# Attention stage of a fused decoder step: low parts on VectorE, cache pages in pairs, prompt transposes one step later

## The chip, the cores and the metric

The kernel runs on one core of a Trainium2 chip. A core has TensorE (PE; its weight loads are listed as PEld), VectorE (DVE), ScalarE (ACT) and GpSimd (POOL), and the DMA queues that SyncE (SP), ScalarE and GpSimd issue to. The metric is the device time of one execution in microseconds.

## The reference, cut to what matters

One step of a two-layer decoder trunk, for a prompt of 512 tokens and for 8 sampled sequences of 8 tokens each, with the same weights. Layer 0 projects the normalised input into five parts; a gating MLP uses two of them, differential attention the other three:

```
p = h @ w_in                      # u, v (gating MLP), q, k, vb (4 heads x 128)
s1 = q[..., :64] @ k[..., :64].T  # two score maps per head
s2 = q[..., 64:] @ k[..., 64:].T
a  = softmax(s1) - lam * softmax(s2)
o  = rmsnorm(a @ vb, attn_subln) * (1 - lam_init)
```

The prompt attends causally to itself. Each sampled sequence attends to 1024 past tokens, whose keys and values lie in a paged cache (8 pages of 128 tokens for each of 8 sequences, found through a page table), and to its own new tokens. Then come an output projection, a SwiGLU, and layer 1 with a diagonal state space model, a GLU and another SwiGLU.

## The kernel before

All 576 tokens (512 prompt, 64 sample) lie along the free axis. A projection is a list of units; a unit is 128 output columns. Its fp32 weights are split into a high and a low part: ScalarE rounds the tile (`wh`, line 260), and VectorE or GpSimd subtracts that from the tile (`wl`, line 263). Each product is then three matmuls into `acc` (line 278): high by high, low by high, high by low. `Stream.splits` prepares two units ahead, and the set `GLO` names the units whose subtraction GpSimd does: unit 0 and units 6 to 27. Units 0 to 19 are the layer's input projection, 20 to 27 the half of the output projection that needs the MLP part, 28 to 35 the half that needs attention.

Attention is woven into this stream. Each unit's matmul loop yields some four times; at each yield the `Driver` ticks, and every side generator then advances by its pace: `sample_attn` by `SP0 = 1.9` steps a tick from unit 4 on, `prompt_attn` by one step from unit 10 on. What a generator emits in a step enters the program there; the framework then orders each engine's instructions by that program order and a plan of when their inputs are ready. Each engine works through its order in sequence.

`sample_attn` walks over `order`: key passes (`keys`) and value passes (`values`) for four pairs of sequences. GpSimd gathers pages (line 725), five ahead, into six buffers `pg`. A key page is transposed by TensorE into a bank `ktp` (line 780), copied to `kt` by ScalarE or VectorE in turn (lines 783, 785), and scored two pages later (`lag`, `LAG = 2`; line 761, `ssc`) in four 128x32 tiles of the array, one for each head. Each score takes eight matmul instructions, as fp32 matmuls are issued in two. A value page is multiplied in the same four tiles (line 847, `so`). `soft` makes the weights of a pair, `finish` the normed heads; `side_step` advances these every second page.

`prompt_attn` works on 16 blocks (4 heads, 4 row blocks): `probs` (scores `S`, masks, Exp), one step later `weights` (VectorE's `p`, lines 647 to 650, and then at once TensorE's transposes `AT`, line 653, and ScalarE's copy), one step later `values` (`O`), and after a head's last block `normed`, whose square is GpSimd's (line 667) and whose product with `sub_b` is VectorE's (line 672). `v_rows` applies Gelu to a part of `v` and transposes it into the banks `vtm` and `vts` (lines 908, 909).

All these small results share four PSUM banks; `acc` has four of its own.

Of the kernel before, what the change touches and what calls it, by code (L numbers as in the profile page):

```python
# [12 lines left out]
AF = mybir.ActivationFunctionType  # L13
ALU = mybir.AluOpType
AX = mybir.AxisListType

P = 128
# [12 lines left out]
LAG = 2  # L30
# [4 lines left out]
CUTS = ((0, 4), (4, 8))  # L35
KSPL = 3
NPIN = 4
GLO = frozenset((0, *range(6, 28)))
SP0, SP1, SP2, SP3 = 1.9, 1.0, 1.0, 1.0
FPARTS = ((0, 6), (6, 6), (12, 6), (18, 4))  # L40


# [35 lines left out]
def kernel(ctx, tc, I, O, stop=None, dbg=None):  # L78
    nc = tc.nc
    V, A, G, PE, SP = nc.vector, nc.scalar, nc.gpsimd, nc.tensor, nc.sync  # L80
# [30 lines left out]
    def bank(name, shape=(P, 512)):  # L111
        return ps.tile(list(shape), F32, tag="bank", name=nm(name))
# [20 lines left out]
    ident = const("ident", [P, P])  # L133
# [364 lines left out]
    sub_b = const("sub_b", [P, P])  # L498
# [126 lines left out]
    def prompt_attn(heads):  # L625
        def probs(h, i):
            n = P * (i + 1)
            es = []
            sums = small("sums", 2)
            for e in range(2):  # L630
                sp = bank("S")
                PE.matmul(sp[:, 0:n], lhsT=qT[h][64 * e:64 * e + 64, P * i:P * i + P],
                          rhs=kT[h][64 * e:64 * e + 64, 0:n], start=True, stop=True)
                V.tensor_tensor(sp[:, n - P:n], sp[:, n - P:n], cmask, op=ALU.add)
                m = small("m", 1)
                V.reduce_max(m, sp[:, 0:n], axis=AX.X)
                nmx = small("nmx", 1)
                V.tensor_scalar(nmx, m, -0.125, None, op0=ALU.mult)
                p = blk("p", (P, 512))
                A.activation(p[:, 0:n], sp[:, 0:n], AF.Exp, bias=nmx, scale=0.125, accum_out=sums[:, e:e + 1])  # L640
                es.append(p)
            return es, sums

        def weights(i, es, sums):
            n = P * (i + 1)
            rc = small("rc", 2)
            V.reciprocal(rc, sums)
            V.tensor_tensor(rc[:, 1:2], rc[:, 1:2], neglam, op=ALU.mult)
            V.tensor_scalar(es[1][:, 0:n], es[1][:, 0:n], rc[:, 1:2], None, op0=ALU.mult)
            V.scalar_tensor_tensor(es[0][:, 0:n], es[0][:, 0:n], rc[:, 0:1], es[1][:, 0:n], op0=ALU.mult, op1=ALU.add)  # L650
            tp = bank("AT")
            for j in range(i + 1):
                PE.transpose(tp[:, P * j:P * j + P], es[0][:, P * j:P * j + P], ident)
            at = blk("at", (P, 512))
            A.copy(at[:, 0:n], tp[:, 0:n])
            return at

        def values(h, i, at, o):
            op = bank("O")
            for j in range(i + 1):  # L660
                PE.matmul(op[:, 0:P], lhsT=at[:, P * j:P * j + P], rhs=Vh[h][:, j, :],
                          start=(j == 0), stop=(j == i))
            V.tensor_copy(o[:, P * i:P * i + P], op[:, 0:P])

        def normed(h, o):
            sq = blk("osq", (P, 512))
            G.tensor_tensor(sq, o, o, op=ALU.mult)
            ss = small("oss", 4)
            V.tensor_reduce(ss, sq.rearrange("p (i d) -> p i d", i=4), axis=AX.X, op=ALU.add)
            r = rstd_from(ss, 4, P)  # L670
            o4 = o.rearrange("p (i d) -> p i d", i=4)
            V.tensor_tensor(o4, o4, sub_b.unsqueeze(1).to_broadcast([P, 4, P]), op=ALU.mult)
            V.tensor_tensor(o4, o4, r.unsqueeze(2).to_broadcast([P, 4, P]), op=ALU.mult)

        def out(h, o):
            tp = bank("oTp")
            for i in range(4):
                PE.transpose(tp[:, P * i:P * i + P], o[:, P * i:P * i + P], ident)
            ao[4 + h] = split_to(h, slice(0, NP), tp)

        todo = [(h, i) for h in heads for i in range(4)]
        pr, at, o = {}, {}, {}
        for t in range(len(todo) + 6):
            if t < len(todo):
                pr[t] = probs(*todo[t])
                yield
            if 0 <= t - 1 < len(todo):
                at[t - 1] = weights(todo[t - 1][1], *pr.pop(t - 1))
                yield
            if 0 <= t - 2 < len(todo):  # L690
                h, i = todo[t - 2]
                if i == 0:
                    o[h] = blk("o", (P, 512))
                while Vh[h] is None:
                    yield
                values(h, i, at.pop(t - 2), o[h])
                if i == 3:
                    normed(h, o[h])
                yield
            if 0 <= t - 4 < len(todo) and todo[t - 4][1] == 3:  # L700
                h = todo[t - 4][0]
                out(h, o.pop(h))
                yield


    def sample_attn():
# [23 lines left out]
        todo = []  # L730
# [12 lines left out]
        sc, at, side_ = {}, {}, []  # L743
# [27 lines left out]
        def keys(bp):  # L771
            for c in range(2):
                for j in range(4):
                    for b2 in range(2):
                        if len(lag) == LAG:
                            score(*lag.pop(0))
                        pgt = page()
                        tp = bank("ktp")
                        for h in range(4):
                            PE.transpose(tp[:, P * h:P * h + P], pgt[:, P * h:P * h + P], ident)  # L780
                        kt = ablk("kt", (P, 512))
                        if b2 == 0:
                            A.copy(kt, tp)
                        else:
                            V.tensor_copy(kt, tp)
                        lag.append((bp, c, j, b2, kt))
                        yield
                    side_step()

        def soft(bp):  # L790
# [40 lines left out]

        def values(bp):
            while bp not in at:
                if lag:
                    score(*lag.pop(0))
                side_step()
                yield
            w = at.pop(bp)
            for b2 in range(2):
                b = 2 * bp + b2  # L840
                ob = bank("so")
                for j in range(8):
                    vp = page()
                    if lag:
                        score(*lag.pop(0))
                    for h in range(4):
                        PE.matmul(ob[32 * h:32 * h + 32, 0:P], lhsT=w[:, 64 * j + 16 * h:64 * j + 16 * h + 32],  # L847
                                  rhs=vp[:, P * h:P * h + P], start=(j == 0), stop=(j == 7), tile_position=(0, 32 * h))
                    if j % 2 == 1:
                        side_step()  # L850
                    yield
                A.copy(OS[b // 4][:, b % 4, :], ob[:, 0:P])
            if bp % 2 == 1:
                side_.append(finish(bp // 2))

        def finish(n):
            while "done" not in smp:
                yield
            o = OS[n]
            ob = bank("son")  # L860
            for j in range(4):
                b = 4 * n + j
                for h in range(4):
                    PE.matmul(ob[32 * h:32 * h + 32, P * j:P * j + P], lhsT=atn[:, b // 2, 16 * h:16 * h + 32],
                              rhs=smp["Vs"][:, h, :], start=True, stop=True, tile_position=(0, 32 * h))
                if j == 1:
                    yield
            V.tensor_tensor(o.rearrange("p a b -> p (a b)"), o.rearrange("p a b -> p (a b)"), ob, op=ALU.add)
            yield
            sq = ablk("osq", (P, 4, P))  # L870
            G.tensor_tensor(sq, o, o, op=ALU.mult)
            ss = small("oss", 4)
            V.tensor_reduce(ss, sq, axis=AX.X, op=ALU.add)
            G.tensor_tensor(o, o, sub_b.unsqueeze(1).to_broadcast([P, 4, P]), op=ALU.mult)
            r = rstd_from(ss, 4, P)
            V.tensor_tensor(o, o, r.unsqueeze(2).to_broadcast([P, 4, P]), op=ALU.mult)
            yield
            yield
            tp = bank("soT")
            for j in range(4):  # L880
                PE.transpose(tp[:, P * j:P * j + P], o[:, j, :], ident)
            for h in range(4):
                split_to(h, slice(NP + 32 * n, NP + 32 * n + 32), tp)
# [12 lines left out]
    def v_rows(f):  # L896
# [4 lines left out]
        yield  # L901
        gv = vT[f]
        A.activation(gv, gv, AF.Gelu_apprx_tanh)
        yield
        yield
        tp, tq = bank("vtm"), bank("vts")
# [1021 lines left out]
```

## Time and profile before

| | before |
|---|---|
| median of 3 runs | 1450.46 us (1450.17 to 1450.61) |
| the profiled execution | 1450.84 us, span 1449.1 us |
| busy over the span | PE 96%, PEld 91%, DVE 57%, ACT 33%, POOL 16% |
| mean granted clock of TensorE | 0.984 of full speed |

A span is what the trace covers; the profiled execution took 1.7 us more than its span. Busy shares are averages over stages with different limits. The end of a matmul is modelled and matmuls overlap, so the time that a group of them holds TensorE is read from one start to the next, not from their durations. A wait names the instruction that waited, and what ended its wait.

### The profile page before, as it was taken

To read this page: it belongs to the slowest core of one execution; us is meant where nothing else is said; L and a number is where in the kernel's file an instruction comes from. 1 tells how busy PE (TensorE), PEld (TensorE's weight loads), DVE (VectorE), ACT (ScalarE), POOL (GpSimd) and SP (SyncE) were. 2 spreads that over 40 slices of the span, in tenths; PEclk is the share of its full clock that TensorE was granted. 3 is DMA by queue.
4 is the path that set the end of the run, shared out by engine and by line. 5 is a ranking of instruction groups with operands and counts; after the bars stand their busy time and mean duration, and the time that the engine had idled before them with its cause. 6 is when DMAs were issued, how large, how long until landed. Compare 5 with 4: busy or idle time off the path is not lost. (4 is left out here: it accounts for less than half of the span.)

```text
span 1449.1 us, 27653 instructions
## 1 busy us (share of the span) xinstructions
PE 1392.5 (96%) x11382; PEld 1316.6 (91%) x11382; DVE 829.9 (57%) x1955; ACT 479.6 (33%) x860; POOL 232.8 (16%) x250
## 2 busy tenths in 40 slices
PE   7999999988999999999999979999999999999997
PEld 6878777868899999999998978999999999999997
DVE  6433456557689744987983478544444444444455
ACT  4233455442422123233322345433222222222234
POOL 2565656552200000000000110010000000000002
PEclk9999999999999999999999989999999999999999
DMA  7566544353332433454457485233223322322411
GB/s 240 168 196 193 172 146 134 110 183 106 96 85 66 146 88 79 138 164 123 143 144 218 128 259 183 67 88 85 62 74 98 92 66 81 88 81 70 114 59 66
DMA packets 223557, 177.37 MB, mean 122 GB/s; under 512 B 34060, under 2 KB 199752, under 8 KB 223432
## 3 DMA queue, kind: packets, MB, share of 16 engines
q1 hardware_dynamic: 206312, 136.01, 32.4%
q0 software_dynamic: 10880, 35.66, 8.2%
q10 hardware_dynamic: 6240, 3.93, 0.9%
q8 instruction: 90, 1.47, 0.4%
q14 instruction: 35, 0.29, 0.1%
HBM read 154.24 MB, written 25.53 MB: 124 GB/s over the span
## 5 line engine op out<-in xcount | busy, mean ns | idle before, releaser
L278 PE MATMUL acc<-hi,wh 128*128 128x288 f32 x2432 | 724.3, 298 | 9.3 <-ACT wh L260 3.1
L278 PE MATMUL acc<-hi,wl 128*128 128x288 f32 x2432 | 719.3, 296 | 1.5 <-DVE wl L263 1.4
L278 PE MATMUL acc<-lo,wh 128*128 128x288 f32 x2432 | 718.7, 296 | 0.5 <-DVE lo L228 0.5
L278 PEld LDWEIGHTS acc<-hi,wh 128*128 128x128 f32 x2432 | 458.2, 189 | 16.6 <-ACT hi L227 4.9
L278 PEld LDWEIGHTS acc<-hi,wl 128*128 128x128 f32 x2432 | 458.6, 189 | 3.1 <-DVE wl L263 2.4
L278 PEld LDWEIGHTS acc<-lo,wh 128*128 128x128 f32 x2432 | 458.8, 189 | 1.8 <-issue 1.0
L260 ACT CAST wh<-raw 128x1024 fp32r<-128x1024 f32 (+2 forms) x196 | 184.9, 945 | 594.8 <-PE acc L278 405.8
L263 DVE TENSOR_TENSOR wl<-raw,wh 128x1024 fp32r<-128x1024 f32 (+2 forms) x173 | 191.7, 1108 | 52.6 <-ACT wh L260 51.9
L1114 DVE TENSOR_TENSOR tu<-acc,rb 128x288 f32<-128x288 f32 x88 | 40.1, 456 | 124.7 <-PE acc L278 124.6
L278 PE MATMUL acc<-gxh,wh 128*128 128x288 f32 x320 | 102.3, 323 | 0.9 <-DVE proj L372 0.9
L991 POOL TENSOR_TENSOR acc<-acc,sq 128x576 f32<-128x576 f32 x18 | 26.8, 1489 | 460.8 <-ACT sq L983 460.8
L278 PE MATMUL acc<-gxl,wh 128*128 128x288 f32 x320 | 97.3, 305 | 0.0
L278 PE MATMUL acc<-gxh,wl 128*128 128x288 f32 x320 | 96.5, 304 | 0.6 <-DVE wl L263 0.6
L1104 DVE TENSOR_TENSOR tg<-acc,rb 128x288 f32<-128x288 f32 x88 | 40.0, 456 | 97.2 <-PE acc L278 96.2
L1124 DVE TENSOR_TENSOR x<-acc,x 128x288 f32<-128x288 f32 x96 | 43.8, 457 | 73.4 <-PE acc L278 73.0
L1834 POOL TENSOR_TENSOR sq<-sq,sq 128x288 f32<-128x288 f32 x12 | 9.6, 803 | 431.2 <-ACT sq L1830 431.2
L725 POOL DMA_INDIRECT pg<-in_cache_k_dram,pidx x64 | 61.9, 966 | 61.0 <-PE ktp L780 24.6
L725 POOL DMA_INDIRECT pg<-in_cache_v_dram,pidx x64 | 64.3, 1004 | 44.1 <-PE so L847 14.0
L278 PEld LDWEIGHTS acc<-gxh,wh 128*128 128x128 f32 x320 | 61.8, 194 | 8.8 <-issue 8.1
L278 PEld LDWEIGHTS acc<-gxl,wh 128*128 128x128 f32 x320 | 62.2, 195 | 1.9 <-issue 1.6
L278 PEld LDWEIGHTS acc<-gxh,wl 128*128 128x128 f32 x320 | 61.5, 193 | 1.9 <-DVE wl L263 0.8
L263 POOL TENSOR_TENSOR wl<-raw,wh 128x1024 fp32r<-128x1024 f32 (+1 forms) x23 | 46.8, 2035 | 39.0 <-ACT wh L260 38.7
(441 smaller groups left out, 1522.6 us busy)
## 6 DMA issues: line engine op xcount, KB each, us to landing
raw<-in_w_ffn_in_dram SPq DMA_DIRECT2D x88, 512.0 KB
raw<-in_w_ffn_out_dram SPq DMA_DIRECT2D x24, 768.0 KB
raw<-in_w_in_even_dram SPq DMA_DIRECT2D x10, 1024.0 KB
raw<-in_w_glu_dram SPq DMA_DIRECT2D x16, 512.0 KB
raw<-in_w_out_even_dram SPq DMA_DIRECT2D x8, 512.0 KB
dF<-Fn SPq DMA_DIRECT2D x16, 256.0 KB
dG<-gt SPq DMA_DIRECT2D x16, 256.0 KB
dL<-dZ SPq DMA_DIRECT2D x64, 64.0 KB
```

Of the source, the lines that this page charges most:

```text
L260: c = A.copy(hi[:, 0:nk], src)
L263: c = (lo_eng or V).tensor_tensor(lo[:, 0:nk], src, f32(hi[:, 0:nk]), op=ALU.subtract)
L278: PE.matmul(pts[hf], lhsT=w[:, k, :], rhs=x[:, c0:c1], start=(k == 0 and wi == 0), stop=(k == nk - 1 and wi == 2))
L725: G.indirect_dma_start(out=t, out_offset=None, in_=src, in_offset=bass.IndirectOffsetOnAxis(ap=pidx[:, 8 * b + j:8 * b + j + 1], axis=0))
L991: G.tensor_tensor(self.acc[:, 0:NT], self.acc[:, 0:NT], q, op=ALU.add)
L1104: V.tensor_tensor(half(t, hf), pt, half(stat.need(), hf), op=ALU.mult)
L1114: V.tensor_tensor(half(t, hf), pt, half(stat.need(), hf), op=ALU.mult)
L1124: V.tensor_tensor(half(nxt[m], hf), pt, half(cur[m], hf), op=ALU.add)
L1834: G.tensor_tensor(acc[h], acc[h], q, op=ALU.add)
```

## The change

`GLO` shrinks to unit 0, so VectorE makes the low parts of units 6 to 27. `SP0` becomes 0.95, and each step of `keys` and `values` handles two pages: `keys` first scores all that is in `lag`, then transposes two pages; `values` multiplies two pages before it yields. In `prompt_attn` the transposes leave `weights` for a function `turned` that runs one step later, and `values`, `normed` and `out` move one step back with it. The squares in `normed` and `finish` go from GpSimd to ScalarE, the product with `sub_b` in `finish` from GpSimd to VectorE. `v_rows` yields once more before its transposes.

```
-GLO = frozenset((0, *range(6, 28)))
-SP0, SP1, SP2, SP3 = 1.9, 1.0, 1.0, 1.0
+GLO = frozenset((0,))
+SP0, SP1, SP2, SP3 = 0.95, 1.0, 1.0, 1.0
...
             V.scalar_tensor_tensor(es[0][:, 0:n], es[0][:, 0:n], rc[:, 0:1], es[1][:, 0:n], op0=ALU.mult, op1=ALU.add)
+            return es[0]
+
+        def turned(i, e):
+            n = P * (i + 1)
             tp = bank("AT")
             for j in range(i + 1):
-                PE.transpose(tp[:, P * j:P * j + P], es[0][:, P * j:P * j + P], ident)
+                PE.transpose(tp[:, P * j:P * j + P], e[:, P * j:P * j + P], ident)
             at = blk("at", (P, 512))
             A.copy(at[:, 0:n], tp[:, 0:n])
             return at
...
         def normed(h, o):
             sq = blk("osq", (P, 512))
-            G.tensor_tensor(sq, o, o, op=ALU.mult)
+            A.activation(sq, o, AF.Square)
...
-        for t in range(len(todo) + 6):
+        for t in range(len(todo) + 7):
...
             if 0 <= t - 1 < len(todo):
-                at[t - 1] = weights(todo[t - 1][1], *pr.pop(t - 1))
+                we[t - 1] = weights(todo[t - 1][1], *pr.pop(t - 1))
+            if 0 <= t - 2 < len(todo):
+                at[t - 2] = turned(todo[t - 2][1], we.pop(t - 2))
                 yield
-            if 0 <= t - 2 < len(todo):
-                h, i = todo[t - 2]
+            if 0 <= t - 3 < len(todo):
+                h, i = todo[t - 3]
...
         def keys(bp):
             for c in range(2):
                 for j in range(4):
+                    while lag:
+                        score(*lag.pop(0))
                     for b2 in range(2):
-                        if len(lag) == LAG:
-                            score(*lag.pop(0))
                         pgt = page()
...
                         lag.append((bp, c, j, b2, kt))
-                        yield
+                    yield
                     side_step()
...
         def values(bp):
             while bp not in at:
-                if lag:
+                while lag:
                     score(*lag.pop(0))
...
                     vp = page()
-                    if lag:
+                    while lag:
                         score(*lag.pop(0))
...
                     if j % 2 == 1:
                         side_step()
-                    yield
+                        yield
...
             sq = ablk("osq", (P, 4, P))
-            G.tensor_tensor(sq, o, o, op=ALU.mult)
+            A.activation(sq, o, AF.Square)
...
-            G.tensor_tensor(o, o, sub_b.unsqueeze(1).to_broadcast([P, 4, P]), op=ALU.mult)
+            V.tensor_tensor(o, o, sub_b.unsqueeze(1).to_broadcast([P, 4, P]), op=ALU.mult)
...
         A.activation(gv, gv, AF.Gelu_apprx_tanh)
+        yield
         yield
         yield
```

## Rows read from the trace of the kernel before

**Rows 1.** The page, part 1: busy us, share of the span, instructions.
```profile
PE 1392.5 (96%) x11382; PEld 1316.6 (91%) x11382; DVE 829.9 (57%) x1955; ACT 479.6 (33%) x860; POOL 232.8 (16%) x250
```

**Rows 2.** Two stretches: length, busy us by engine, clock, DMA share, GB/s.
```profile
130.00:320.00 190.00, 177.84 (x1725) 141.43 (x1725) 100.06 (x334) 87.57 (x205) 115.83 (x105) 0.96 0.51 155
320.00:350.00 30.00, 25.27 (x205) 22.79 (x206) 26.28 (x85) 7.22 (x15) 10.08 (x9) 1.00 0.47 139
```

**Rows 3.** TensorE's waits from 70 to 400 us: total, times, longest.
```profile
PE so L847 <- DMA pg<-in_cache_v_dram,pidx: 4.0, 2, 3.5
PE vts L909 <- ACT p L640: 2.6, 1, 2.6
...
PE sh L944 <- issue: 2.0, 1, 2.0
...
PE AT L653 <- DVE p L650: 1.4, 1, 1.4
```

**Rows 4.** Timeline of TensorE, two stretches: start us, us, instructions merged.
```profile
166.07 0.29 PE L278 MATMUL acc<-gxl,wh 128*128 128x288 f32 x1
166.21 0.29 PE L278 MATMUL acc<-gxh,wl 128*128 128x288 f32 x1
166.43 0.43 PE L761 MATMUL ssc<-kt,Qz 128*32 128x128 f32 x8
166.79 0.66 PE L780 MATMUL ktp<-ident,pg 128*128 128x128 f32 x4
...
194.06 0.65 PE L847 MATMUL so<-pg,sat 128*32 128x128 f32 x16
194.63 0.40 PE L278 MATMUL acc<-gxh,wh 128*128 128x288 f32 x1
```

**Rows 5.** Timeline of TensorE: first and last of 63 score runs, 44 value runs.
```profile
55.67 0.43 PE L761 MATMUL ssc<-kt,Qz 128*32 128x128 f32 x8
...
122.06 0.43 PE L847 MATMUL so<-pg,sat 128*32 128x128 f32 x8
...
258.21 0.40 PE L761 MATMUL ssc<-kt,Qz 128*32 128x128 f32 x8
...
319.31 0.43 PE L847 MATMUL so<-pg,sat 128*32 128x128 f32 x8
```

**Rows 6.** Three stretches with a lower granted clock (third figure from the right).
```profile
200.00:208.00 8.00, 8.00 (x49) 7.07 (x51) 1.73 (x5) 2.10 (x11) 1.93 (x2) 0.57 0.30 83
272.00:280.00 8.00, 8.00 (x41) 7.81 (x39) 0.70 (x1) 2.09 (x5) 1.29 (x1) 0.57 0.24 70
306.00:310.00 4.00, 3.04 (x18) 2.67 (x19) 0.00 (x0) 0.00 (x0) 3.08 (x4) 0.57 1.01 378
```

**Rows 7.** Timeline from 192 us, VectorE and GpSimd.
```profile
192.27 3.32 DVE L672 TENSOR_TENSOR o<-o,sub_b 128x512 f32<-128x512 f32 x1
192.64 2.40 POOL L263 TENSOR_TENSOR wl<-raw,wh 128x1024 fp32r<-128x1024 f32 x1
```

**Rows 8.** Groups by shape, 60 to 420 us: busy us, mean ns, idle before.
```profile
L263 POOL TENSOR_TENSOR wl<-raw,wh 128x1024 fp32r<-128x1024 f32 x14 | 33.5, 2390 | 7.3 <-ACT wh L260 7.1
L263 POOL TENSOR_TENSOR wl<-raw,wh 128x512 fp32r<-128x512 f32 x8 | 11.0, 1374 | 19.8 <-ACT wh L260 19.8
...
L263 DVE TENSOR_TENSOR wl<-raw,wh 128x1024 fp32r<-128x1024 f32 x6 | 7.3, 1222 | 2.4 <-ACT wh L260 2.4
L263 DVE TENSOR_TENSOR wl<-raw,wh 128x512 fp32r<-128x512 f32 x8 | 5.5, 694 | 0.1
L672 DVE TENSOR_TENSOR o<-o,sub_b 128x512 f32<-128x512 f32 x4 | 5.4, 1342 | 0.0
```

**Rows 9.** Timeline of GpSimd from 299 us.
```profile
300.09 1.30 POOL L263 TENSOR_TENSOR wl<-raw,wh 128x512 fp32r<-128x512 f32 x1
```

**Rows 10.** Groups by shape, 0 to 60 us: ScalarE's square over 128x512.
```profile
L404 ACT ACTIVATE junk<-xt 128x512 f32<-128x512 f32 x6 | 3.9, 643 | 0.0
```

**Rows 11.** Timeline of ScalarE's queue from 316 us.
```profile
335.26 5.36 ACTq L1263 DMA_DIRECT2D dZ<-zz x7
```

More of the change, by code (lines that the diff above doesn't have):

```diff
@@ L37 @@
 NPIN = 4
-GLO = frozenset((0, *range(6, 28)))
-SP0, SP1, SP2, SP3 = 1.9, 1.0, 1.0, 1.0
+GLO = frozenset((0,))
+SP0, SP1, SP2, SP3 = 0.95, 1.0, 1.0, 1.0
 FPARTS = ((0, 6), (6, 6), (12, 6), (18, 4))
@@ L650, in weights, with turned @@
             V.scalar_tensor_tensor(es[0][:, 0:n], es[0][:, 0:n], rc[:, 0:1], es[1][:, 0:n], op0=ALU.mult, op1=ALU.add)
+            return es[0]
+        def turned(i, e):
+            n = P * (i + 1)
             tp = bank("AT")
             for j in range(i + 1):
-                PE.transpose(tp[:, P * j:P * j + P], es[0][:, P * j:P * j + P], ident)
+                PE.transpose(tp[:, P * j:P * j + P], e[:, P * j:P * j + P], ident)
             at = blk("at", (P, 512))
@@ L666, in normed @@
             sq = blk("osq", (P, 512))
-            G.tensor_tensor(sq, o, o, op=ALU.mult)
+            A.activation(sq, o, AF.Square)
             ss = small("oss", 4)
@@ L681, in prompt_attn @@
         todo = [(h, i) for h in heads for i in range(4)]
-        pr, at, o = {}, {}, {}
-        for t in range(len(todo) + 6):
+        pr, we, at, o = {}, {}, {}, {}
+        for t in range(len(todo) + 7):
             if t < len(todo):
@@ L687, in prompt_attn @@
             if 0 <= t - 1 < len(todo):
-                at[t - 1] = weights(todo[t - 1][1], *pr.pop(t - 1))
+                we[t - 1] = weights(todo[t - 1][1], *pr.pop(t - 1))
+            if 0 <= t - 2 < len(todo):
+                at[t - 2] = turned(todo[t - 2][1], we.pop(t - 2))
                 yield
-            if 0 <= t - 2 < len(todo):
-                h, i = todo[t - 2]
+            if 0 <= t - 3 < len(todo):
+                h, i = todo[t - 3]
                 if i == 0:
@@ L695, in prompt_attn @@
                     yield
-                values(h, i, at.pop(t - 2), o[h])
+                values(h, i, at.pop(t - 3), o[h])
                 if i == 3:
@@ L699, in prompt_attn @@
                 yield
-            if 0 <= t - 4 < len(todo) and todo[t - 4][1] == 3:
-                h = todo[t - 4][0]
+            if 0 <= t - 5 < len(todo) and todo[t - 5][1] == 3:
+                h = todo[t - 5][0]
                 out(h, o.pop(h))
@@ L773, in keys @@
                 for j in range(4):
+                    while lag:
+                        score(*lag.pop(0))
                     for b2 in range(2):
-                        if len(lag) == LAG:
-                            score(*lag.pop(0))
                         pgt = page()
@@ L786, in keys @@
                         lag.append((bp, c, j, b2, kt))
-                        yield
+                    yield
                     side_step()
@@ L833, in values @@
             while bp not in at:
-                if lag:
+                while lag:
                     score(*lag.pop(0))
@@ L843, in values @@
                     vp = page()
-                    if lag:
+                    while lag:
                         score(*lag.pop(0))
@@ L850, in values @@
                         side_step()
-                    yield
+                        yield
                 A.copy(OS[b // 4][:, b % 4, :], ob[:, 0:P])
@@ L870, in finish @@
             sq = ablk("osq", (P, 4, P))
-            G.tensor_tensor(sq, o, o, op=ALU.mult)
+            A.activation(sq, o, AF.Square)
             ss = small("oss", 4)
             V.tensor_reduce(ss, sq, axis=AX.X, op=ALU.add)
-            G.tensor_tensor(o, o, sub_b.unsqueeze(1).to_broadcast([P, 4, P]), op=ALU.mult)
+            V.tensor_tensor(o, o, sub_b.unsqueeze(1).to_broadcast([P, 4, P]), op=ALU.mult)
             r = rstd_from(ss, 4, P)
@@ L903, in v_rows @@
         A.activation(gv, gv, AF.Gelu_apprx_tanh)
+        yield
         yield
```

## Prediction

> **What bounds the kernel.** I read the page first. TensorE is busy 96% of the span [rows 1], so only work that leaves its queue, or time in which it stands still, can pay. What the change touches runs from about 60 to 350 us; what comes later is the same code. The table of stretches [rows 2] shows three kinds of loss there. From 130 to 350 us TensorE stands idle for 190.00 - 177.84 + 30.00 - 25.27 = 16.9 us. Its clock is 0.96 in the first of the two. And GpSimd is busy 115.83 of 190 us, while VectorE has 100 of 190 and then 26.28 of 30: the only place where an engine beside TensorE is nearly full.
>
> The list of waits [rows 3] says what the larger stops wait for. `so` waits 4.0 us for a value page, `vts` 2.6 us for an Exp, `sh` 2.0 us for nothing that the list can name, `AT` (the prompt transposes) 1.4 us for the weights `p`. That is 10 us of the 16.9; the rest are stops under a microsecond.
>
> The timeline [rows 4] shows a loss that no wait shows, because TensorE counts as busy in it. Full-array matmuls start 0.14 us apart, but a group of scores (128x32 tiles) after one starts 0.22 us behind it: 0.08 to enter. A group of eight (one page) holds the queue 166.79 - 166.43 = 0.36 us, a group of sixteen (two pages) 194.63 - 194.06 = 0.57. Eight more cost 0.21, so 0.15 of the 0.36 is leaving. One trip into the small tiles and back is 0.08 + 0.15 = 0.23 us.
>
> **Pages in pairs.** How many trips? In the timeline of the whole stage the 64 pages' scores stand in 63 runs and the 64 value pages in 44; [rows 5] shows the first and the last run of each. A few touch one another, which leaves 102 trips with the few other small-tile runs. After the change a step scores two pages and then transposes two, and a value step takes two. Halving the pace to 0.95 keeps pages per tick. That makes 32 + 32 trips, and I add 4 for the small runs of `soft` and `finish`: 68, 34 fewer, 34 x 0.23 = 7.8 us off. Bounds: if only the key pages pair up (63 to 35), 28 x 0.23 = 6.4; if neighbours also merge (102 to 58), 10.1. I take 7.8, as value pages already ran in sixteens at times.
>
> [...]
>
> **Low parts off GpSimd.** 22 of the 23 subtractions on GpSimd go to VectorE: 14 of 2.390 us and 8 of 1.374 [rows 8], 44.5 us. On VectorE the same shapes take 1.222 and 0.694 [rows 8]: 17.1 + 5.6 = 22.7 us added. What this removes beyond GpSimd's time stands in [rows 7]: VectorE's product with `sub_b` took 3.32 us while GpSimd worked from 192.64 to 195.04. The four of that group average 1.342 [rows 8], so the other three took (4 x 1.342 - 3.32) / 3 = 0.68. The 2.6 us lost held up the next masks and Exp, which held the bank that `vts` needed: this is the 2.6 us wait of [rows 3]. Behind it the granted clock falls to half; the 8 us stretch at 200 us has a mean of 0.57 [rows 6], so 8 x 0.43 = 3.4 us are lost. Together 6.0 us hang on it. VectorE's and ScalarE's order around it will also change, and a bank must still be waited for; bounds 0 and 6.0, I take 4.
>
> [...]
>
> The value page: at 300.09 a subtraction of 1.30 us [rows 9] stands in GpSimd's queue ahead of the gathers that follow, and a page that TensorE then lacks makes the longest stop of [rows 3], 3.5 of the 4.0 us, with a half clock behind it (4 x 0.43 = 1.7 us, [rows 6]). Without the subtraction those gathers go 1.3 us earlier; bounds 0 and 4.0 + 1.7 = 5.7, I take 1.3. I leave the `sh` stop and its clock (2.0 + 3.4, [rows 3, 6]) as it is: nothing in the change speaks to its cause. Bounds 0 and 5.4.
>
> **What VectorE pays.** It is covered by TensorE's matmuls up to 320 us, where VectorE has 90 of 190 us free. Two things can uncover it. A subtraction must wait for ScalarE's cast, and in VectorE's queue the page copies `kt`, the score masks and the evacuations of `acc` stand behind it, and TensorE behind those. The six in [rows 8] waited 2.4 us in all, 0.4 each; 22 would wait 8.8 us of VectorE. And from 320 to 350 us VectorE is 88% busy; if all eight half-size subtractions fall there they add 8 x 0.69 = 5.6 us, and one `sub_b` product 0.7. Bounds 0 and 6.3 + 8.8 = 15; I take 2, since the same GpSimd instructions also stretched VectorE there.
>
> **Squares on ScalarE.** Six squares of 0.64 us [rows 10], 3.9 us, where ScalarE has more than half of 190 us free [rows 2]. Late in the stage there is one trap: ScalarE's queue issues transfers for 5.36 us from 335.26 [rows 11], and a square queued behind them would hold the last head's norm, its transposes and the projection units that need them. Bounds 0 and 5.4; I take 0.5, as TensorE still has other projection units there.
>
> **Transposes a step behind.** The instructions are the same 40 transposes and 16 copies; the wait on `p`, 1.4 us [rows 3], goes. The weights now live one step longer, in a ring of 44 buffers; heads finish one step later, but the number of steps with a yield stays 52. Bounds: 1.4 off, and one step put on at the end, 190 / 52 = 3.7 us if the 52 steps fill the long stretch of [rows 2]. I take 1 off. The extra yield in `v_rows` gives Gelu one step more and moves nothing else; 0, bounds as for the wait on `vts` above.
>
> **Banks.** A key step now wants two banks at once for its transposes, out of four. Lower bound 0; upper, every one of 32 pairs waits for a copy of 0.69 us (the VectorE pass above), 22 us. At a pace of 1.9 a tick already sends two pages through these banks, so I take 1.
>
> **Sum.** -7.8 - 4 - 1.3 - 1 + 2 + 0.5 + 1 = -10.6 us. The profiled execution took 1450.84 us, 1449.1 of it span and 1.7 around it; the median is 1450.46, 0.4 less. 1450.46 - 10.6 = 1439.9; I say **1440**.
>
> **Rivals.**
> 1. The forecast: 1430 to 1447 us, chance 0.55. The trips go and some stops with them.
> 2. The trips go but are given back, in VectorE's last 30 us, behind casts or in a new stop with its half clock: 15 us at most against 14.1 off, so about 1448 to 1452; or the pairs are pulled apart in the instruction order, which leaves the trips and, -10.6 + 7.8 = -2.8, gives 1447.7. For it: VectorE at 88% [rows 2]; against it: 90 us free before. Chance 0.22, three quarters of it above 1447.6.
> 3. Slower: the pair's two banks. With the prompt's scores holding others, the second set of transposes waits for a copy, and TensorE, which works in order, with it. The pairs win 10.6 us in all, so from 10.6 / 32 = 0.33 us a pair on this turns the sign; at 0.69 us a pair it is 1450.5 - 11.6 + 22 = 1461. For it: four banks for all; against it: in [rows 4] the transposes start directly behind the scores. Chance 0.13.
> 4. All the stops named above go as well, with their half clocks: 7.8 + 6.0 + 5.7 + 5.4 + 1.4 = 26 us, 1424. Chance 0.10, mostly between 1424 and 1432.
>
> Faster by over 0.2% (2.9 us, about what a measurement of this kernel can tell from none) means under 1447.6: 0.55 + 0.10 and a quarter of rival 2, 0.70. Within it 0.15, slower 0.15. The range from 1428 to 1452 leaves out most of rival 3 and the end of rival 4; the likeliest case alone has 1430 to 1447.
>
> **What would show it.** Right: scores and values in groups of sixteen, key transposes in eights, near 68 trips; the four `sub_b` products of the prompt all near 0.69 us; one subtraction left on GpSimd; no wait of `AT` on `p`; the projection units that end at 350 us ending near 340. Wrong: as many trips as before, transposes that wait for a `kt` copy, TensorE's idle time from 320 us on growing, or new half-clock stretches. The prediction is most open to the last: a stop of 2 us costs 3.4 more in clock, and where stops fall I can't derive.

## The result and the profile after

The changed kernel takes 1436.82 us (median of 4 runs, 1430.29 to 1438.41) beside 1450.53 for the kernel before (4 runs, 1450.17 to 1451.69): a ratio of 0.9894, 95% interval 0.988 to 0.9909, 13.7 us. A second set of runs (e12 below, on chip 11; the chip of the first set is not on record) gave 1428.39 beside 1445.25, ratio 0.989 [0.9868, 0.9912], 16.9 us. The forecast was 1440 with a range from 1428 to 1452; the rest of this text is about whether its terms were the right ones. The kernel before took 1449.82 us on chip 2 and 1444.64 and 1445.25 on chip 11, so a time is always set against the kernel before of its own set.

The page of the changed kernel, part 1 [against rows 1]:

```profile
PE 1384.8 (97%) x11382; PEld 1317.7 (92%) x11382; DVE 840.3 (59%) x1979; ACT 482.8 (34%) x866; POOL 182.3 (13%) x220
```

GpSimd has 50 us less to do and VectorE only 10 us more, though it took over 44.5 us of GpSimd's subtractions. The stretches of rows 2 in the changed kernel, and before them the one that holds the half clock that is left, 0.50 from 298 to 300 us (length, busy us by engine, clock, DMA share, GB/s):

```profile
296.00:304.00 8.00, 8.00 (x55) 5.40 (x58) 4.22 (x11) 2.27 (x7) 3.15 (x4) 0.79 0.55 168
130.00:320.00 190.00, 181.63 (x1827) 146.91 (x1824) 117.48 (x379) 94.73 (x220) 87.23 (x90) 0.99 0.54 165
320.00:350.00 30.00, 29.67 (x225) 29.30 (x224) 24.53 (x75) 10.26 (x17) 2.86 (x2) 1.00 0.37 115
```

TensorE's idle time from 130 to 350 us is 8.37 + 0.33 = 8.7 us; it was 16.9 [rows 2]. From 130 to 320 us its clock is 0.99 instead of 0.96. The low stretches at 200 and 272 us [rows 6] are gone, and the one at 306 has become 8 us at 0.79. Behind 350 us the clock is no better: its mean from 350 to 420 us is 0.95, and was 0.98. The last transposes `rbp` ahead of the SwiGLU, which both programs have, start at 378.19 us instead of 394.74; the spans of the two profiled executions differ by 14.2 us, so 2.4 of these 16.6 us are lost again later.

TensorE's waits from 70 to 400 us [against rows 3]:

```profile
PE so L853 <- issue: 3.0, 3, 2.3
PE so L853 <- DMA pg<-in_cache_v_dram,pidx: 2.7, 3, 1.0
...
PE AT L657 <- ACT p L640: 1.8, 1, 1.8
PE rowt L464 <- ACT S L772: 1.4, 2, 0.7
```

The waits of `vts` on an Exp, of `sh`, and of `AT` on VectorE's `p` are gone; no wait for a page is longer than 1.0 us. Not all is better: `so` now stands 3.0 us for nothing that the list can name, and `AT` waits 1.8 us for an Exp. New is `rowt`, which waits until ScalarE has copied the score bank `S` out. Timeline of TensorE [against rows 4 and 5]:

```profile
162.27 0.64 PE L767 MATMUL ssc<-kt,Qz 128*32 128x128 f32 x16
162.85 1.09 PE L786 MATMUL ktp<-ident,pg 128*128 128x128 f32 x8
...
184.38 0.65 PE L767 MATMUL ssc<-kt,Qz 128*32 128x128 f32 x16
184.84 0.62 PE L853 MATMUL so<-pg,sat 128*32 128x128 f32 x16
```

Scores come in sixteens and transposes in eights, directly behind them. Counted over the stage there are 73 trips into the small tiles, 29 fewer than the 102 before. Groups by shape from 60 to 420 us [against rows 8 and 10]:

```profile
L263 DVE TENSOR_TENSOR wl<-raw,wh 128x1024 fp32r<-128x1024 f32 x23 | 28.1, 1223 | 5.1 <-ACT wh L260 4.2 <-issue 0.5
...
L263 DVE TENSOR_TENSOR wl<-raw,wh 128x512 fp32r<-128x512 f32 x16 | 11.0, 688 | 1.2 <-ACT wh L260 1.2
...
L676 DVE TENSOR_TENSOR o<-o,sub_b 128x512 f32<-128x512 f32 x4 | 2.7, 682 | 0.0
...
L671 ACT ACTIVATE osq<-o 128x512 f32<-128x512 f32 x4 | 2.5, 628 | 0.6 <-DVE rsy L180 0.6
```

All four products with `sub_b` take 0.68 us; the one of 3.32 [rows 7] is gone. VectorE's idle time before all 39 subtractions is 6.3 us; the prediction's upper bound was 8.8 us for 22 of them.

### The profile page after: what moved, and what is told of

Read it like the earlier page. It is cut to its first block, busy times and chain, and to the rows that moved or that the text cites. A ratio compares the mean times of both kernels' runs of the same rounds, so it can differ in the third digit from the quotient of the medians.

```text
span 1434.9 us, 27625 instructions
## 1 busy us (share of the span) xinstructions
PE 1384.8 (97%) x11382; PEld 1317.7 (92%) x11382; DVE 840.3 (59%) x1979; ACT 482.8 (34%) x866; POOL 182.3 (13%) x220
## 5 line engine op out<-in xcount | busy, mean ns | idle before, releaser
L263 DVE TENSOR_TENSOR wl<-raw,wh 128x1024 fp32r<-128x1024 f32 (+2 forms) x195 | 214.1, 1099 | 56.1 <-ACT wh L260 54.4
L227 ACT CAST hi<-tu 128x576 fp32r<-128x576 f32 x44 | 29.8, 677 | 41.9 <-DVE tu L1123 41.9
```

The source lines that it names most:

```text
L227: A.copy(hi, src)
L263: c = (lo_eng or V).tensor_tensor(lo[:, 0:nk], src, f32(hi[:, 0:nk]), op=ALU.subtract)
```

## The experiments

In the first four, theory A is the prediction's (the saved trips bring most of the gain), theory B that the work taken off GpSimd does. e1 to e4 ran on chip 2, all later ones on chip 11.

**e1, pairs alone.** The kernel before with the new `keys` and `values` and `SP0 = 0.95`.

```
-SP0, SP1, SP2, SP3 = 1.9, 1.0, 1.0, 1.0
+SP0, SP1, SP2, SP3 = 0.95, 1.0, 1.0, 1.0
...
+                    while lag:
+                        score(*lag.pop(0))
                     for b2 in range(2):
-                        if len(lag) == LAG:
-                            score(*lag.pop(0))
```

> The kernel before with the pairs and the pace of 0.95 alone. In its instruction order the small-tile trips fall from 102 to 71. Theory A (a trip costs TensorE 0.23 us whatever else happens): 31 x 0.23 = 7.1 us off, about 1443.4 us, with the stop of vts and its half clock perhaps still there. Theory B (the trips lie in time that TensorE would have waited anyway, and the gain came from GpSimd's work leaving): within 2 us of 1450.5.

1463.4 us beside 1449.82, ratio 1.0087 [1.0067, 1.0107]: 13.6 us slower, which neither theory said. It makes 71 trips, 31 fewer than before, and gives back more than they save. Where? The stretches of the kernel before (first fence) and of e1:

```profile
60.00:130.00 70.00, 69.16 (x724) 56.78 (x724) 22.12 (x56) 23.63 (x42) 44.39 (x42) 1.00 0.59 176
```

```profile
60.00:130.00 70.00, 63.31 (x686) 56.49 (x684) 20.82 (x47) 21.33 (x36) 39.68 (x37) 0.98 0.53 165
130.00:320.00 190.00, 168.14 (x1633) 136.74 (x1634) 101.53 (x333) 87.40 (x205) 109.28 (x100) 0.94 0.47 146
320.00:350.00 30.00, 26.13 (x259) 20.68 (x259) 18.01 (x56) 7.37 (x18) 17.02 (x17) 0.96 0.54 168
```

TensorE idles 6.7 us from 60 to 130 (0.8 before) and 21.9 + 3.9 = 25.7 from there to 350 (16.9 before), and its clock is lower in all three. There are two kinds of stop. The first, in e1's timeline of several engines from 82 us, happens three times:

```profile
82.21 0.66 PE L761 MATMUL ssc<-kt,Qz 128*32 128x128 f32 x16
...
82.80 1.09 PE L780 MATMUL ktp<-ident,pg 128*128 128x128 f32 x8
...
83.73 0.60 PE L462 MATMUL rows<-ident,proj 128*128 128x128 f32 x4
...
84.08 0.38 PE L278 MATMUL acc<-gxh,wh 128*128 128x288 f32 x1
85.31 0.69 DVE L764 TENSOR_REDUCE mx<-ssc 128x1 f32<-128x512 f32 x1 [2.92 <-PE acc L278]
...
86.04 0.59 ACT L766 COPY S<-ssc 128x512 f32<-128x512 f32 x1 [4.54 <-issue]
...
86.68 0.42 PE L464 MATMUL rowt<-ident,proj 128*64 128x128 f32 x1 [2.21 <-ACT S L766]
```

`ssc`, two `ktp` and `rows` hold the four banks, so `rowt` waits for the score bank: reduced by VectorE, then copied by ScalarE. The reduction starts 2.4 us after the scores' end. VectorE was idle for 2.92 us up to it, and by its line a signal of TensorE ended this wait (`PE acc`). Five groups of TensorE, the scores first and one `acc` last, end between 82.87 and 84.46 us by the modelled ends, and neither VectorE nor ScalarE starts anything until 85.31. So the reduction was late with TensorE's signal; why that came so long after the modelled ends is not shown. The second kind, in e1's timeline around 250 us, VectorE, GpSimd and TensorE in this order:

```profile
249.50 0.69 DVE L873 TENSOR_REDUCE oss<-osq 128x4 f32<-128x512 f32 x1 [1.16 <-POOL osq L871]
...
250.47 3.78 DVE L186 TENSOR_SCALAR var<-oss 128x4 f32<-128x4 f32 x1
...
256.35 0.28 DVE L663 COPY o<-O 128x128 f32<-128x128 f32 x1
```

```profile
250.63 1.29 POOL L874 TENSOR_TENSOR OS<-OS,sub_b 128x512 f32<-128x512 f32 x1
251.87 2.34 POOL L263 TENSOR_TENSOR wl<-raw,wh 128x1024 fp32r<-128x1024 f32 x1
```

```profile
251.65 0.29 PE L278 MATMUL acc<-gxh,wh 128*128 128x288 f32 x1
256.69 0.72 PE L908 MATMUL vtm<-ident,proj 128*128 128x128 f32 x4 [4.75 <-DVE o L663]
```

A VectorE instruction over four columns, 0.16 us in the changed kernel, takes 3.78 us and ends 0.04 us after the two GpSimd instructions that run beside it. The copy of `O` stands behind it and eleven short instructions, and `vtm` waits for that copy's bank: TensorE stands for 4.75 us.

**e2, the GpSimd work moved and nothing else.** Low parts, squares and products, in the kernel before.

```
-GLO = frozenset((0, *range(6, 28)))
+GLO = frozenset((0,))
...
-            G.tensor_tensor(sq, o, o, op=ALU.mult)
+            A.activation(sq, o, AF.Square)
...
-            G.tensor_tensor(o, o, sub_b.unsqueeze(1).to_broadcast([P, 4, P]), op=ALU.mult)
+            V.tensor_tensor(o, o, sub_b.unsqueeze(1).to_broadcast([P, 4, P]), op=ALU.mult)
```

> The kernel before with the low parts, squares and the sub_b product off GpSimd alone; trips 105. Theory A: +0.7 for three trips, -5.3 for the stops of vts and of the value page, +2.5 for VectorE and ScalarE: about 1448 us. Theory B: most of the 13.7 us, 1440 us or less.

1434.45 us beside 1449.82, ratio 0.9891 [0.9871, 0.9911]: 15.4 us, as much as the whole change, with as many trips as before (105). B. Its stretches:

```profile
130.00:320.00 190.00, 183.00 (x1823) 145.66 (x1823) 119.88 (x389) 94.75 (x220) 89.32 (x88) 0.99 0.52 161
320.00:350.00 30.00, 29.73 (x220) 29.41 (x219) 21.49 (x64) 10.03 (x16) 2.60 (x2) 0.96 0.43 133
```

Idle time 7.00 + 0.27 = 7.3 us, 9.6 less than before [rows 2]; the clock of the first goes from 0.96 to 0.99, 5.7 us, and that of the second to 0.96, 1.2 us the other way. 9.6 + 5.7 - 1.2 = 14.1 of the 15.4, an estimate from these rows. VectorE is busy 119.88 us in the long stretch instead of 100.06, and the wait of `vts` on an Exp is gone from e2's list.

**e3, the later transposes alone.** `turned` and the extra yield of `v_rows` in the kernel before.

```
-                at[t - 1] = weights(todo[t - 1][1], *pr.pop(t - 1))
+                we[t - 1] = weights(todo[t - 1][1], *pr.pop(t - 1))
+            if 0 <= t - 2 < len(todo):
+                at[t - 2] = turned(todo[t - 2][1], we.pop(t - 2))
```

> The kernel before with the prompt's transposes one step later and the extra yield alone; trips 100. Theory A: the 1.4 us wait of AT goes and two trips with it, about 1449 us. Theory B: the same; a gain of over 4 us would speak for neither, but for the step as the cause.

1445.87 us beside 1449.82, ratio 0.9969 [0.9957, 0.9981]: 4.0 us faster, where both theories said about 1449. The waits of `AT` on VectorE are gone from its list of waits, and so is that of `vts`: though GpSimd still makes the low parts, none of the four products with `sub_b` is stretched here (0.68 us on average). So the 4.0 us are not those of the wait on `p` alone.

**e4, pairs pulled apart again.** The changed kernel, but a key step scores a page, transposes one, scores the other, transposes the other.

```
-                    while lag:
-                        score(*lag.pop(0))
                     for b2 in range(2):
+                        if len(lag) == LAG:
+                            score(*lag.pop(0))
```

> The changed kernel, a step still two pages at the same pace, but a key step emits score, transposes, score, transposes, with the scores two pages behind as before. Trips 97 in place of 73, nothing else changed. Theory A: 24 x 0.23 = 5.5 us more than the changed kernel, about 1442.3 us. Theory B: as the changed kernel, 1436.8 within its spread (1430 to 1438).

1439.89 us beside the changed kernel's 1436.8, ratio to the kernel before 0.9927 [0.9909, 0.9945]: 3.1 us for 24 more trips (97), between A and B. A trip is worth 3.1 / 24 = 0.13 us here, not 0.23. The two kernels ran on different occasions and their intervals touch, so the 0.13 is rough.

With these four the question became why pairs alone lose 13.6 us, when the whole change holds the same pairs. Theories A and B are new from here, as the texts say.

**e6, the change without the pairs**, and **e7, the change without the later transposes** (so: pairs and the moved GpSimd work).

```
-SP0, SP1, SP2, SP3 = 0.95, 1.0, 1.0, 1.0
+SP0, SP1, SP2, SP3 = 1.9, 1.0, 1.0, 1.0
```

> The changed kernel with single pages again (pace 1.9, a score two pages behind its transposes); everything else of the change stays. Theory A (the low parts and products on GpSimd were what made the pairs lose: they make VectorE late, and so the banks come free late; without them the pairs are worth their trips): single pages cost 3 to 5 us again, 1440 to 1442. Theory B (the pairs lose in the banks whatever GpSimd does): the two other parts add up, 1449.8 - 15.4 - 4.0 = 1430.4.

> The kernel before with the pairs and with GpSimd's work moved, but without the later transposes of the prompt and of v. Theory A (GpSimd's work was what made the pairs lose): the 13.6 us of the pairs are gone, so 1434 to 1440. Theory B (banks alone): the two add up, 1449.8 + 13.6 - 15.4 = 1448.

e6: 1432.17 us, ratio 0.9924 [0.9898, 0.9949]. e7: 1425.91 us, ratio 0.9879 [0.9854, 0.9904]. The kernel before took 1444.64 on this chip, so the texts' sums shift by -5.2. For e7 B then gives 1442.8 and A 1429 to 1435; it is below both: with GpSimd's work moved, no loss from the pairs is seen on this chip, where pairs alone did not run. For e6 B gives 1425.2 and A 1435 to 1437; it lies between, nearer to A: pairs are now worth something, if less than their trips were priced at. A in the main.

**e10, pairs alone with five banks**, and **e11, the kernel before with five banks.**

```
-    pm = ctx.enter_context(tc.tile_pool(name="pm", bufs=4, space=bass.MemoryType.PSUM))
-    ps = ctx.enter_context(tc.tile_pool(name="ps", bufs=4, space=bass.MemoryType.PSUM))
+    pm = ctx.enter_context(tc.tile_pool(name="pm", bufs=3, space=bass.MemoryType.PSUM))
+    ps = ctx.enter_context(tc.tile_pool(name="ps", bufs=5, space=bass.MemoryType.PSUM))
```

> Pairs alone, with five banks for the small results and three for acc instead of four and four. If banks are what the pairs wait for (B): the 13.6 us lost come back, and some of the trips with them, 1450 or less after what three acc banks cost (the control run beside it tells that). If the pairs lose because pages and VectorE's work come late (A): 1463 plus that cost.

> Control: the kernel before with five banks for the small results and three for acc. Both theories: within 4 us of 1449.8, as acc needs two banks for a unit and the kernel before had few waits for banks. A gain over 4 us would say that banks bound the kernel before as well.

e10: 1439.29 us, ratio 0.9965 [0.9948, 0.9981], where e1 had 1.0087. e11: 1441.83, ratio 0.9984 [0.9963, 1.0005]. A fifth bank brings the kernel before little (its interval holds 1), and with five banks the pairs gain 2.5 us, with intervals that overlap. Set against e1 this is 18 us by the ratios, B's number; but e1 ran on chip 2 and e10 on chip 11. In e10's stretch from 60 to 130 us the stops of `rowt` are gone:

```profile
60.00:130.00 70.00, 70.00 (x758) 62.45 (x755) 24.94 (x70) 24.73 (x50) 47.08 (x43) 1.00 0.63 193
```

That the fifth bank removed them is not shown. The changed kernel was traced in the first set and again on chip 11 (e12), and there too the first reduction starts late in the one and at once in the other; timelines of the first set, then of e12:

```profile
67.64 0.65 PE L767 MATMUL ssc<-kt,Qz 128*32 128x128 f32 x16
69.14 0.69 DVE L770 TENSOR_REDUCE mx<-ssc 128x1 f32<-128x512 f32 x1 [1.89 <-PE ktp L786]
```

```profile
66.45 0.64 PE L767 MATMUL ssc<-kt,Qz 128*32 128x128 f32 x16
67.16 0.69 DVE L770 TENSOR_REDUCE mx<-ssc 128x1 f32<-128x512 f32 x1 [1.09 <-PE ssc L767]
```

The same program has 0.85 us between the scores' end and the reduction in the one trace and 0.07 in the other, and TensorE stands idle 1.97 and 0.00 us from 60 to 130 us. Of the eight score passes the first four lie before 120 us. There every trace of chip 11 has 0.07, with GpSimd's work or without, with four banks or five. On chip 2 it is 0.07 to 0.54 us in e2 and e4, where GpSimd's work is moved, 0.26 to 2.16 in e3 and 2.40 to 2.49 in e1, where it is not. So the chip, or the occasion, is a rival to the fifth bank, and to a part of what e7 shows. Pairs alone, with four banks, on chip 11 would decide; that was not run.

Without chip 11 this much can be said: if the parts of e1, e2 and e3 added up, the whole change would take 1449.8 + 13.6 - 15.4 - 4.0 = 1444.0 us, and it took 1436.8 in the first set, beside a kernel before that is 0.7 us slower there. So at least half of the pairs' loss is not there in the whole change, and e7, without the later transposes, points to the moved work: A. B stays open.

**e12, e13, e14, e8 on one chip.** e12 is the changed kernel again, e13 is e2 again, e14 is e7 again; e8 is the changed kernel with the old `GLO`, squares and products staying where the change puts them.

```
-GLO = frozenset((0,))
+GLO = frozenset((0, *range(6, 28)))
```

> The changed kernel itself, beside the next three on one chip. Its ratio to the kernel before was 0.9894 [0.988, 0.9909]; both theories below: the same again.

> GpSimd's work moved and nothing else (e2), beside the changed kernel and e14. Theory A (with GpSimd's work moved, pairs are worth their trips): slower than e14 by 3 us or more. Theory B (pairs bring nothing either way; the waits for pages take back what the trips give): within 2 us of e14.

> GpSimd's work moved, and pairs (e7), without the later transposes. Theory A: faster than e13 by 3 us or more. Theory B: within 2 us of it. On the later transposes: if they are worth their 4.0 us (e3) here too, 4 us slower than the changed kernel; if they only had a wait on VectorE to remove that the moved work removes as well, equal to it or faster.

> The changed kernel with the low parts of units 6 to 27 on GpSimd again; squares and products stay on ScalarE and VectorE. If GpSimd's subtractions are what hold VectorE up, and with it the banks (A): 12 us or more slower than the changed kernel. If the squares and the sub_b products were (B): within 3 us of it.

| | median us (range) | ratio to the kernel before (1445.25) |
|---|---|---|
| e13: GpSimd work moved | 1430.19 (1427.27 to 1436.76) | 0.9907 [0.9882, 0.9932] |
| e14: and pairs | 1425.68 (1425.45 to 1427.42) | 0.987 [0.9849, 0.9891] |
| e12: and later transposes (the change) | 1428.39 (1425.17 to 1432.53) | 0.989 [0.9868, 0.9912] |
| e8: the change, low parts back on GpSimd | 1434.18 (1427.27 to 1441.69) | 0.9929 [0.9904, 0.9955] |

Pairs are worth 4.5 us on top of the moved work (much the same by e6 against the change: 0.9924 to 0.989, 4.9 us), with intervals that just overlap. On the first sets there is no such gain: e2, without pairs, has 0.9891 on chip 2, and the whole change 0.9894. The later transposes, 4.0 us alone, cost 2.7 on top of the rest; that is near what can be told apart, but the 4 us are not there. The low parts account for 5.8 us, measured beside pairs and later transposes, where the moved work of e13 gave 15.1; this lies between A's 12 and B's 3. The intervals of e8 and e12 overlap a little, and the size is uncertain by about as much. The other 9 would then be the six squares and two products, but only if the parts add up: it is a difference and not a run of its own.

e14's timeline where e1 stalled, before its first `rowt`, and its stretches and longest wait:

```profile
66.22 0.65 PE L761 MATMUL ssc<-kt,Qz 128*32 128x128 f32 x16
...
66.80 1.09 PE L780 MATMUL ktp<-ident,pg 128*128 128x128 f32 x8
66.93 0.69 DVE L764 TENSOR_REDUCE mx<-ssc 128x1 f32<-128x512 f32 x1 [1.09 <-PE ssc L761]
...
67.66 0.59 ACT L766 COPY S<-ssc 128x512 f32<-128x512 f32 x1 [2.36 <-DVE mx L764]
...
68.30 0.30 PE L464 MATMUL rowt<-ident,proj 128*64 128x128 f32 x1
```

```profile
60.00:130.00 70.00, 70.00 (x771) 62.55 (x768) 31.03 (x70) 24.60 (x47) 36.02 (x37) 1.00 0.62 197
130.00:320.00 190.00, 182.66 (x1856) 151.21 (x1855) 125.06 (x405) 96.01 (x219) 86.81 (x87) 0.98 0.54 167
```

```profile
PE so L847 <- DMA pg<-in_cache_v_dram,pidx: 6.2, 7, 1.6
```

Four banks and pairs as in e1, but on chip 11; the reduction starts 0.06 us after the scores end and `rowt` waits for nothing. The largest wait is now the page supply: 6.2 us, where e13's list has 2.8. It takes back a part of what the trips give.

e14 (and e7, the same kernel) is the fastest measured: 2.7 us below the change on one chip, 0.2%, with overlapping intervals. It beats the kernel before beyond doubt, the changed one probably.

## Why the prediction came out near, and which step was wrong

The size was right and the largest term was not; that the sum came within 3.2 us of the first set was in part luck, as a term that was too large made up for one that was too small. The sum gave 7.8 us to trips and 2.8 net to the work taken off GpSimd (-4 - 1.3 + 2 + 0.5). Measured, the moved work alone brings 15.4 and 15.1 us, and the pairs alone lose 13.6 on chip 2. The step that failed is the pricing of the GpSimd work, in three places; how the 15 us divide among them is not shown.

- **"Squares on ScalarE", +0.5.** Priced as six more instructions for ScalarE. What was not priced is who waits for a square on GpSimd: VectorE's reduction, and everything behind it in VectorE's queue. The list of VectorE's waits had it; kernel before, then e1, then the changed kernel (total us, times, longest):

```profile
DVE oss L669 <- POOL osq L667: 2.7, 3, 1.7
...
DVE oss L873 <- POOL osq L871: 2.0, 2, 1.5
```

```profile
DVE oss L669 <- POOL osq L667: 8.1, 4, 4.3
...
DVE oss L873 <- POOL osq L871: 1.2, 1, 1.2
```

```profile
DVE oss L673 <- ACT osq L671: 1.4, 2, 1.2
```

  4.7 us of VectorE standing still before, 9.3 with pairs, 1.4 after. The prediction works from TensorE's waits and not from VectorE's, though two terms of its sum go by way of VectorE.
- **"What VectorE pays", +2.** The subtractions cost TensorE nothing visible: its idle time in the last stretch fell from 4.73 to 0.33 us [rows 2]. VectorE there was 88% busy in part with instructions that were stretched beside GpSimd's: four over 128x4 took 0.95 to 1.23 us, where most others of that shape took 0.14 to 0.17, and each of the four ends 0.02 us after a GpSimd subtraction; it is at 24.53 of 30 us now, with the added work in the stage. One of the four in the timeline of the kernel before, and the GpSimd instruction that ends 0.02 us ahead of it:

```profile
341.75 0.98 DVE L186 TENSOR_SCALAR var<-oss 128x4 f32<-128x4 f32 x1
341.41 1.30 POOL L263 TENSOR_TENSOR wl<-raw,wh 128x512 fp32r<-128x512 f32 x1 [0.45 <-ACT wh L260]
```

- **The `vts` stop, -4.** The reading fits: the 3.32 us product, the late Exp and the half clock behind it [rows 6, 7] are all gone, and in e3, where the product is short though GpSimd keeps the low parts, the stop is gone as well. But it was one of several such places and was priced as the only one.

The value page, -1.3, can't be read out of the runs. The waits of `so` for pages fell from 4.0 to 2.7 us, but it has a new stop of 3.0 us, and a half clock of the same worth as before is left (8 x 0.21 = 1.7 us at 296, 4 x 0.43 = 1.7 at 306).

How GpSimd's work stretches an instruction of VectorE is not shown. The product of 3.32 us [rows 7] has two inputs, e1's instruction of 3.78 us one. By the records the latter started 0.16 us before the first of the two GpSimd instructions and ended 0.04 us after the second.

**Pages in pairs, -7.8.** The trips went nearly as forecast, 29 in the change and 31 in e1 of the 34. Their value was mis-sized: 4.5 us for the 35 trips between e13 (105) and e14 (70) is 0.13 each, as by e4; by e6 and e12 it is 4.9 us for 31, 0.16. 0.23 was read from the one place that was looked at. Pages then come later than TensorE wants them (6.2 us of waits in e14), which takes part of it back.

**Banks, +1, and rival 3.** The third rival came true in e1 in its sign and its size (it had 1461 us at worst for the whole change, e1 took 1463.4), but not by its mechanism: `ktp` waits 0.5 us in e1's whole list, while `rowt` stands 6.7 us for the score bank, `vtm` 4.7 for the copy of `O` and `oTp` 3.7 behind `var`. In the change these stops are small: `rowt` 2.2 us in all, and neither `vtm` nor `oTp` is on its list of waits. The prediction added the parts up as if each kept its price beside the others; by the sum of e1, e2 and e3 they don't, by 7 us.

**Transposes a step behind, -1.** The wait on `p` went. Alone the step is worth 4.0 us on chip 2; beside the moved work and the pairs on chip 11 nothing, or a little less than nothing.

**What stays open.** Why the reduction starts up to 2.49 us after the modelled end of TensorE's scores in some traces (e1) and 0.07 us after it in others (e12). Whether the pairs alone lose 13.6 us on any chip but chip 2, and whether a fifth bank would bring that back there. The split between low parts and squares is uncertain by several microseconds, and squares alone were not run.

## What to carry to other kernels

Work on a side engine is priced by who waits for its results, and by what it does to its neighbour's instructions: read the waits of every engine through whose queue the critical one is fed, not of the critical engine alone. Parts of a change that share buffers and engines need not add up: run such parts alone and together, and all of them on one chip. A sum that comes out right may hold two wrong terms.

## What the runs showed of the hardware that was not expected

A VectorE instruction over 128x4 elements, with a single input, took 3.78 us instead of 0.16 beside two GpSimd instructions. A trip of TensorE into small-tile matmuls and back cost 0.13 to 0.16 us net, measured by whole kernels, where one place in a timeline gave 0.23. The same program started the reduction of its first scores 0.85 us after their modelled end in one set of runs and 0.07 us after it in another.
